# Two more quads with seven products in each ssm pass, left factors laid ready, and side transfers moved to ScalarE's and GpSimd's queues

## The chip, the core and the metric

The kernel runs on one core of a Trainium2 chip. A core has a matrix engine (TensorE, in profiles PE, its weight loads PEld), a vector engine (VectorE, DVE), a scalar engine (ScalarE, ACT), a general one (GpSimd, POOL) and a queue engine (SyncE, SP), which only issues transfers. Transfers (DMA) between device memory and on-chip memory can be issued from SP, ScalarE or GpSimd. Each engine takes its instructions in the order in which the compiler laid them, and waits where one needs another engine's or a transfer's result.

The metric is the device time of one execution in microseconds (us); lower is better.

## The reference

One layer of a hybrid block: 256 tokens, model width 2048, all in 32-bit floats. Cut to what matters here:

```python
hn = rms_norm(x, norm_w)
proj = hn @ w_in          # q k v z_a | z_s (4096) | xbc (6144) | dt (64) | g_a g_s
...                       # 16 heads of dilated attention -> o_a (256 x 2048)
xbc = silu(causal_depthwise_conv(xbc, conv_w, conv_b))
xs, bm, cm = split(xbc)   # xs: 64 heads of 64; bm, cm: 8 groups of 128
...                       # chunked scan over two chunks of 128 tokens -> y (256 x 4096)
y = rms_norm(y * silu(z_s), ssm_norm_w)
merged = sigmoid(g_a) * (o_a @ w_attn_branch) + sigmoid(g_s) * (y @ w_ssm_branch)
return rms_norm(x + merged @ w_out, final_norm_w)
```

The product `y @ w_ssm_branch` (256 x 4096 by 4096 x 2048) is what is meant by the ssm branch below.

## The kernel before, in words

All weights lie in device memory as one list of 481 *units* (`wall`), each 128 x 1024 floats, in the order of use (`weight_plan`). A unit is loaded by SP into a ring of five buffers (`w`), and then split into a high part `h` (ScalarE rounds it to the matrix engine's format, L276) and a low part `l` (VectorE subtracts, L277), four buffers each. A product of two split numbers takes three matmuls (high by high, high by low, low by high): a *triple*.

The stages in order: the first projections with the norm of x; then eight *groups* `g` of the ssm part. A group projects B and C (2 units each) and four pairs of xs and zs (2 units each), 20 units in all. Behind the projections run, with lags counted in *ticks* (one per projection of 2 units), the group's convolution, its `turn` (transposes of xs), four `decays` (each loads a broadcast of cumulated decays into the one buffer `acb` and fills a quarter of `gt`), and the `scan` (32 matmuls into `yp`, L820), after which `gather` puts the result into `yT`. Then come two passes of the ssm branch, two passes of v, the 16 attention heads (q, k, za), and two passes each for ga, attn and out.

A *pass* (`gemm_pair`) yields 1024 output columns. It walks over the inner dimension in *quads*: two blocks of 128 rows by two blocks of 512 columns, two weight units. The ssm passes have 16 quads, the others 8. A quad is done either plainly (24 matmuls of 128x512) or by Strassen's way with seven products (21 matmuls). `S_QUADS` names the latter. Such a quad needs
- sums and differences of the weights: T2 = B22 - (B12 - B11) and so on. Part of it (`wt`) can be made ahead: in `sum_jobs`, `get` loads a unit and a half unit of the quad, `add` makes two subtractions on VectorE (L252, L253), and `spill` stores the result to device memory (`presum`). The pass then loads `wt` (512 KB), `wa` (512 KB) and `wc` (256 KB). Otherwise the pass loads the second unit as `wb` and makes both differences itself (L549, L555). Quad 12 of both ssm passes is always done so (`IN_PLACE`).
- sums and differences of the left factor (`turn_x`): made ahead by `keep_left`, stored as `lefts`, and loaded again by `fetch_left` into an `sx` tile; or, for the quads of `Y_LATE`, made within the first ssm pass (`left_y`). Quads that both passes do with seven products store three of the four (`spare`).

For each seven quad ScalarE rounds four tiles (L543), and VectorE takes four differences of 1024 and one of 512 elements (L544, L557).

`behind_unit(n, f)` runs `f` right after unit n has been split. Before the change, each side transfer (a load of sums, of left factors, of constants) was tied to that place by a one-element copy on GpSimd (`gp.tensor_copy(dst[:, 0:1], behind)`, L247, L251, L432, L638, L903), which needs the unit's `h` and the free destination; SP (or ScalarE for the last loads of x and of the final weights) then issued the transfer. Stores by `spill` were SP's too. 18 differences fitted in the projections, at units 2, 9 and 16 of the groups 1 to 6 and made 3 units later: 13 for the ssm passes, 5 for v; four quads of the second v pass had none.

The compiler's scheduler lays the final order on each engine, by priorities and a timeline that it models; `high_priority(n)` puts an instruction n places ahead. `issue_after(ins)`, which the change uses, lets the instructions within follow `ins` on its engine, without a wait.

Of the kernel before, what the change touches and what calls it, by code (L numbers as in the profile page):

```python
# [15 lines left out]
P = 128  # L16
# [20 lines left out]
DT_LAG, CB_LAG, TURN_LAG, GT_LAG, Y_LAG, S_LAG, M_LAG = 2, 5, 3, 2, 11, 2, 2  # L37
# [3 lines left out]
V_ORDERS = {0: (0, 2, 4, 1, 3, 5, 6, 7), 2: (0, 2, 1, 4, 3, 5, 6, 7)}  # L41
# [6 lines left out]
    ("ssm", 0): (5, 7, 8, 10, 11, 12, 13), ("ssm", 2): (3, 5, 7, 8, 10, 11, 12, 13),  # L48
# [3 lines left out]
Y_ORDERS = {0: (0, 1, 2, 3, 5, 4, 7, 8, 6, 10, 11, 9, 12, 14, 13, 15), 2: (0, 3, 1, 5, 2, 7, 8, 4, 10, 11, 6, 12, 9, 13, 14, 15)}  # L52
Y_LATE = {12: 4, 13: 6}
# [9 lines left out]
SUM_UNITS = 2, 9, 16  # L63
# [133 lines left out]
def hybrid_block(ctx: ExitStack, tc: tile.TileContext, wall, xt, x, pk_d, cst_d, fw_d, out):  # L197
# [33 lines left out]

    def behind_unit(n, f):
        on_unit.setdefault(n, []).append(f)
# [4 lines left out]
    def spill(kept, key, name, src, shape):  # L238
        kept[key] = dram.tile([P, *shape], F32, name=name, tag=name)
        nc.sync.dma_start(kept[key], src)  # L240

    def sum_jobs(jobs, units, places):

        def get(tag, q, t, b11, behind):
# [5 lines left out]
        def add(tag, q, t, b11, res, behind):  # L250
            gp.tensor_copy(res[:, 0:1], behind)  # L251
            ve.tensor_tensor(res[:, :512], t[:, :512], b11, ALU.subtract)  # L252
            ve.tensor_tensor(res[:, 512:], t[:, 512:], res[:, :512], ALU.subtract)  # L253
            spill(presum, (tag, q), f"t_{tag[0]}{tag[1]}_{q}", res, [UNIT])

        for n, ((tag, q), u) in enumerate(zip(jobs, units)):
            t, b11, res = places[n % len(places)]
            behind_unit(u, lambda behind, a=(tag, q, t, b11): get(*a, behind))
            behind_unit(u + SUM_LAG, lambda behind, a=(tag, q, t, b11, res): add(*a, behind))
# [7 lines left out]
    def unit(n, shape):  # L267
# [6 lines left out]
        with tc.high_priority(L_AHEAD) if n >= KT // UB else nullcontext():  # L274
            for a, b in zip(cuts, cuts[1:]):
                ac.activation(h[:, a:b], w[:, a:b], AF.Copy)  # L276
                ve.tensor_tensor(l[:, a:b], w[:, a:b], h[:, a:b].bitcast(F32), ALU.subtract)  # L277
# [151 lines left out]
    def fetch_left(kept, pool, bufs, key, x, spare, u):  # L429
        def get(behind):  # L430
            sx = new_sx(pool, bufs, spare, f"{key[0]}{key[1]}")
            gp.tensor_copy(sx[:, 0, 0, 0:1], behind)  # L432
            nc.sync.dma_start(sx.bitcast(F32), lefts[key])
            kept[key[1]] = left_parts(sx, x, spare)
# [250 lines left out]
    with tc.tile_pool(name="ssm", bufs=2) as sp:  # L685
# [205 lines left out]
        for c in GS_BEFORE[0]:  # L891
# [3 lines left out]
        at = sums_at[:, 3]  # L895
# [3 lines left out]
            [(sums_at[:, 0], sums_at[:, 2, :512], sums_at[:, 1])],  # L899
        )  # L900

        def left_x(q, behind):
            gp.tensor_copy(at[:, 0:1], behind)  # L903
            keep_left(("x", q), two_kts(XT, q), 0, at)
# [4 lines left out]
        for g in range(GROUPS):  # L909
# [55 lines left out]
    xk = ctx.enter_context(tc.tile_pool(name="xk", bufs=1))  # L965
    sx_of_x = {}

    for n, q in enumerate(SX_X[:1]):
        fetch_left(sx_of_x, xk, 1, ("x", q), two_kts(XT, q), 0, plain_unit(("ssm", 2), 12, Y_ORDERS[2]))
# [7 lines left out]
    with tc.tile_pool(name="xp", bufs=1) as xp:  # L977
# [8 lines left out]
        for q in SX_Y:  # L986
            if q in Y_LATE:
                continue
            fetch_left(sxs, xp, sum(s == Y_SPARE[q] for s in Y_SPARE.values()), ("y", q), two_kts(yT, q), Y_SPARE[q], plain_unit(("ssm", 0), Y_ORDERS[0].index(q) - 3 if q in S_QUADS[("ssm", 0)] else 12, Y_ORDERS[0]))
# [24 lines left out]
    behind_unit(FIRST[("v", 2)] + 1, lambda behind: fetch(dc, cst_d[:, :768], behind))  # L1014
# [18 lines left out]
    with tc.tile_pool(name="att", bufs=2) as ap:  # L1033
# [33 lines left out]
        def mix(h, pT, za):  # L1067
# [10 lines left out]
            if h % 2 == 1 and q in ATT_QUADS:  # L1078
                keep_left(("o", q), two_kts(oaT, q), 0, mul.tile([P, UNIT], F32, name=f"sxt_o{q}", tag="ht", bufs=2))
# [3 lines left out]
            [  # L1083
                (th_a[:, i, :UNIT], th_a[:, 1, UNIT + 512 * i : UNIT + 512 * i + 512], th_a[:, 0, UNIT:])
                for i in range(2)
            ],
# [17 lines left out]
        for n, q in enumerate(ATT_QUADS):  # L1104
            fetch_left(
                sx_of_o, xl if n else xk, max(1, n and len(SX_X) - 1), ("o", q), two_kts(oaT, q), 0, FIRST[("ga", 2)] + O_BEHIND[n]
# [9 lines left out]
    with tc.tile_pool(name="fin", bufs=2) as fp:  # L1116
# [36 lines left out]
        for n in range(4):  # L1153
# [3 lines left out]
                lambda behind, i=i, cs=cs: fetch(fin[:, i, cs], x[i * P : (i + 1) * P, cs], behind, nc.scalar),  # L1157
# [3 lines left out]
        for n, (tag, u) in enumerate(FW_BEHIND):  # L1161
            cs = slice(n * UNIT, (n + 1) * UNIT)
            behind_unit(
                FIRST[tag] + u, lambda behind, cs=cs: fetch(fw[:, cs], fw_d[cs].partition_broadcast(P), behind, nc.scalar)
# [107 lines left out]
```

## Time and profile before

| What | us |
|---|---|
| Three runs | 1385.03, 1385.79, 1385.75 |
| Their median | 1385.75 |
| Profiled execution, from the first to the last instruction (span) | 1383.8 |
| Median above that span | 1.95 |
| Ssm passes, first matmul to the first of v | 583.6 to 748.5 |

The profile's page gives each engine's busy time, the span in 40 slices, the transfers by queue, the chain of work that ended last (followed back from the last instruction to what released each step), and the costliest groups of instructions. Other views of the same trace give the busy time in chosen stretches, instructions in order of time, and groups by line and shape. A matmul's record is longer (0.39 us) than the step from one to the next, because matmuls overlap; a busy TensorE can therefore still hide short waits, which show as a longer step. A few per cent of the matmul records may be missing.

### The profile page before, as it was taken

To read this page: it belongs to the slowest core of one execution; us is meant where nothing else is said; L and a number is where in the kernel's file an instruction comes from. 1 tells how busy PE (TensorE), PEld (TensorE's weight loads), DVE (VectorE), ACT (ScalarE), POOL (GpSimd) and SP (SyncE) were. 2 spreads that over 40 slices of the span, in tenths; PEclk is the share of its full clock that TensorE was granted. 3 is DMA by queue.
4 is the path that set the end of the run, shared out by engine and by line. 5 is a ranking of instruction groups with operands and counts; after the bars stand their busy time and mean duration, and the time that the engine had idled before them with its cause. 6 is when DMAs were issued, how large, how long until landed. Compare 5 with 4: busy or idle time off the path is not lost.

```text
span 1383.8 us, 20696 instructions
## 1 busy us (share of the span) xinstructions
PE 1373.6 (99%) x7266; PEld 1169.9 (85%) x7266; DVE 1169.5 (85%) x1753; ACT 835.5 (60%) x1306; POOL 142.0 (10%) x226
## 2 busy tenths in 40 slices
PE   9999999999999999999999999999999999999997
PEld 8888888888888888888888888888888888888886
DVE  7898999987799898789889897777877788888897
ACT  7656677675667675766565554544544556655564
POOL 2301111101011100010001001111111000000112
PEclk9999999999999999999999999999999999999999
DMA  9767988868787866668677668888888757865773
GB/s 347 231 187 225 313 254 291 279 224 287 245 266 240 294 212 208 188 224 280 230 259 267 222 209 278 275 275 273 299 288 301 241 161 264 294 222 180 243 273 122
DMA packets 105080, 345.00 MB, mean 249 GB/s; under 512 B 11728, under 2 KB 13712, under 8 KB 104976
## 3 DMA queue, kind: packets, MB, share of 16 engines
q1 hardware_dynamic: 103536, 339.62, 74.0%
q10 hardware_dynamic: 1440, 4.06, 0.8%
q8 instruction: 57, 0.93, 0.3%
q14 instruction: 47, 0.39, 0.1%
HBM read 314.87 MB, written 28.77 MB: 248 GB/s over the span
## 4 chain that ended last, share of the span: by engine, by line
PE 97%; DMA 1%; DVE 1%; ACT 1%; issue 0%; SPq 0%; POOL 0%; POOLq 0%; DVEq 0%; ACTq 0%
PE ps_zs L329 8%; PE ps_xs L329 8%; PE ps_zs L332 4%; PE ps_q L329 4%; PE ps_za L329 4%; PE ps_k L329 4%; PE ps_xs L332 4%; PE ps_ssm L476 3%; PE ps_ssm L477 3%; PE ps_ssm L478 3%; PE ps_q L332 2%; PE ps_k L332 2%; PE ps_za L332 2%; PE ps_gs L414 2%; PE ps_gs L412 2%; PE ps_gs L413 2%
## 5 line engine op out<-in xcount | busy, mean ns | idle before, releaser
L276 ACT ACTIVATE h<-w 128x1024 fp32r<-128x1024 f32 (+1 forms) x398 | 413.9, 1047 | 318.0 <-issue 78.8
L277 DVE TENSOR_TENSOR l<-w,h 128x1024 fp32r<-128x1024 f32 (+1 forms) x398 | 479.4, 1211 | 124.2 <-ACT h L276 121.8
L329 PE MATMUL ps_zs<-XT,h 128*128 128x512 f32 x496 | 176.3, 397 | 0.0
L329 PE MATMUL ps_xs<-XT,h 128*128 128x512 f32 x496 | 175.9, 396 | 0.0
L332 PE MATMUL ps_zs<-XT,l 128*128 128x256 f32 x496 | 139.9, 282 | 0.0
L332 PE MATMUL ps_xs<-XT,l 128*128 128x256 f32 x496 | 139.8, 282 | 0.0
L329 PEld LDWEIGHTS ps_xs<-XT,h 128*128 128x128 f32 x496 | 93.3, 188 | 21.7
L329 PEld LDWEIGHTS ps_zs<-XT,h 128*128 128x128 f32 x496 | 93.4, 188 | 21.2
L332 PEld LDWEIGHTS ps_zs<-XT,l 128*128 128x128 f32 x496 | 93.7, 189 | 1.5 <-issue 0.7
L332 PEld LDWEIGHTS ps_xs<-XT,l 128*128 128x128 f32 x496 | 93.7, 189 | 0.4
L329 PE MATMUL ps_q<-XT,h 128*128 128x512 f32 x256 | 92.5, 405 | 0.2 <-ACT h L276 0.2
L329 PE MATMUL ps_k<-XT,h 128*128 128x512 f32 x256 | 89.9, 395 | 0.0
L329 PE MATMUL ps_za<-XT,h 128*128 128x512 f32 x256 | 89.7, 394 | 0.0
L543 ACT ACTIVATE ha<-wa 128x1024 fp32r<-128x1024 f32 x43 | 45.4, 1055 | 46.4 <-DMA wa<-in_wall 10.9
L332 PE MATMUL ps_q<-XT,l 128*128 128x256 f32 x256 | 71.2, 278 | 0.0
L332 PE MATMUL ps_k<-XT,l 128*128 128x256 f32 x256 | 71.1, 278 | 0.0
L332 PE MATMUL ps_za<-XT,l 128*128 128x256 f32 x256 | 71.1, 278 | 0.0
L544 DVE TENSOR_TENSOR la<-wa,ha 128x1024 fp32r<-128x1024 f32 x43 | 52.5, 1220 | 11.9 <-ACT ha L543 11.8
L782 ACT ACTIVATE gt<-acb,acT 128x128 f32<-128x128 f32 x128 | 44.2, 391 | 23.7 <-DMA acb<-acum_d 21.9
L329 PEld LDWEIGHTS ps_q<-XT,h 128*128 128x128 f32 x256 | 48.2, 188 | 11.5 <-ACT h L276 0.6
L329 PEld LDWEIGHTS ps_za<-XT,h 128*128 128x128 f32 x256 | 48.1, 188 | 11.3
L329 PEld LDWEIGHTS ps_k<-XT,h 128*128 128x128 f32 x256 | 48.1, 188 | 11.2
(688 smaller groups left out, 3325.1 us busy)
## 6 DMA issues: line engine op xcount, KB each, us to landing
w<-in_wall SPq DMA_DIRECT2D x394, 512.0 KB, 4.7
wa<-in_wall SPq DMA_DIRECT2D x43, 512.0 KB, 4.9
th_a<-in_wall SPq DMA_DIRECT2D x19, 512.0 KB, 5.6
sums_at<-in_wall SPq DMA_DIRECT2D x18, 512.0 KB, 4.7
acb<-acum_d SPq DMA_DIRECT2D x32, 256.0 KB, 4.0
t_ssm<-sums_at SPq DMA_DIRECT2D x13, 512.0 KB, 4.1
wt<-t_ssm SPq DMA_DIRECT2D x13, 512.0 KB, 5.4
th_a<-in_wall SPq DMA_DIRECT2D x19, 256.0 KB, 6.0
```

The lines of the kernel that those rows point to most:

```text
L276: ac.activation(h[:, a:b], w[:, a:b], AF.Copy)
L277: ve.tensor_tensor(l[:, a:b], w[:, a:b], h[:, a:b].bitcast(F32), ALU.subtract)
L329: pe.matmul(acc, h[:, kk, :], m, start=(kt == 0), stop=False)
L332: pe.matmul(acc[:, S:], l[:, kk, :], m[:, :S], start=False, stop=(kt == KT - 1))
L412: pe.matmul(accs[i], xh, h[:, kk], start=(kt == 0), stop=False)
L413: pe.matmul(accs[i], xh, l[:, kk], start=False, stop=False)
L476: pe.matmul(acc, xh, h, start=start, stop=False)
L477: pe.matmul(acc, xh, l, start=False, stop=False)
L478: pe.matmul(acc, xl, h, start=False, stop=stop)
L543: ac.activation(h, src, AF.Copy)
L544: ve.tensor_tensor(l, src, h.bitcast(F32), ALU.subtract)
L782: ac.activation(g4[:, n, b], acb[:, j, b // 2 * P : b // 2 * P + P], AF.Relu, scale=-1.0, bias=sc[:, h : h + 1],)
```

## The change

- The ssm passes do 9 (first) and 10 (second) of their 16 quads with seven products, where they did 7 and 8: quads 6 and 9 are added to both. The orders of the quads are new, also that of the first v pass.
- `sum_jobs` has five places a group instead of three, so all 26 differences of ssm and v are made in the projections. The result is made in the tile into which the unit was loaded (no third tile), and there are two such places.
- Loads of sums, of left factors and of constants are issued by ScalarE (`side`), behind the unit's `h`, and the subtractions follow the unit's `l` on VectorE; the one-element copies on GpSimd go. Stores by `spill` are issued by GpSimd.
- All four left factors of x are fetched at the beginning of the v passes (one had been fetched in the second ssm pass, into a pool of its own).
- The decays of a group come 2, 4, 6 and 9 ticks behind its last xs projection instead of 2, 3, 4 and 9; those of the last group start with the projection before. The last scan comes 4 ticks after the last xs projection (11 before), the one before it 7.

```diff
-DT_LAG, CB_LAG, TURN_LAG, GT_LAG, Y_LAG, S_LAG, M_LAG = 2, 5, 3, 2, 11, 2, 2
+DT_LAG, CB_LAG, TURN_LAG, Y_LAG, S_LAG, M_LAG = 2, 5, 3, 11, 2, 2
+GT_LAGS, END_LAGS, END_LAG = (2, 4, 6, 9), (2, 3, 4, 5), (7, 4)
-V_ORDERS = {0: (0, 2, 4, 1, 3, 5, 6, 7), 2: (0, 2, 1, 4, 3, 5, 6, 7)}
+V_ORDERS = {0: (0, 1, 2, 4, 3, 5, 6, 7), 2: (0, 2, 1, 4, 3, 5, 6, 7)}
-    ("ssm", 0): (5, 7, 8, 10, 11, 12, 13), ("ssm", 2): (3, 5, 7, 8, 10, 11, 12, 13),
+    ("ssm", 0): (5, 6, 7, 8, 9, 10, 11, 12, 13), ("ssm", 2): (3, 5, 6, 7, 8, 9, 10, 11, 12, 13),
-Y_ORDERS = {0: (0, 1, 2, 3, 5, 4, 7, 8, 6, 10, 11, 9, 12, 14, 13, 15), 2: (0, 3, 1, 5, 2, 7, 8, 4, 10, 11, 6, 12, 9, 13, 14, 15)}
-Y_LATE = {12: 4, 13: 6}
+Y_ORDERS = {0: (0, 1, 2, 5, 6, 3, 7, 8, 4, 9, 10, 14, 11, 12, 13, 15), 2: (0, 1, 3, 5, 2, 6, 7, 4, 8, 9, 14, 10, 11, 12, 13, 15)}
+Y_LATE = {12: 3, 13: 4}
-SUM_UNITS = 2, 9, 16
+SUM_UNITS = 1, 5, 9, 13, 17
...
+    def side(dst, src, queue=nc.scalar):
+        with tc.issue_after(here["high"]):
+            queue.dma_start(dst, src)
...
     def spill(kept, key, name, src, shape):
         kept[key] = dram.tile([P, *shape], F32, name=name, tag=name)
-        nc.sync.dma_start(kept[key], src)
+        gp.dma_start(kept[key], src)
...
-            for dst, src in ((t, wall[n + 1]), (b11, wall[n, :, :512])):
-                gp.tensor_copy(dst[:, 0:1], behind)
-                nc.sync.dma_start(dst, src)
+            side(t, wall[n + 1])
+            side(b11, wall[n, :, :512])
...
-            gp.tensor_copy(res[:, 0:1], behind)
-            ve.tensor_tensor(res[:, :512], t[:, :512], b11, ALU.subtract)
-            ve.tensor_tensor(res[:, 512:], t[:, 512:], res[:, :512], ALU.subtract)
-            spill(presum, (tag, q), f"t_{tag[0]}{tag[1]}_{q}", res, [UNIT])
+            with tc.issue_after(here["low"]):
+                ve.tensor_tensor(t[:, :512], t[:, :512], b11, ALU.subtract)
+                ve.tensor_tensor(t[:, 512:], t[:, 512:], t[:, :512], ALU.subtract)
+            spill(presum, (tag, q), f"t_{tag[0]}{tag[1]}_{q}", t, [UNIT])
...
-            [(sums_at[:, 0], sums_at[:, 2, :512], sums_at[:, 1])],
+            [(sums_at[:, n], sums_at[:, 3, n * 512 : n * 512 + 512]) for n in range(2)],
...
+                if t == 4 * GROUPS - 2:
+                    for k in range(4):
+                        after(1 + k, lambda a=(g, k, cb, state): decays(*a))
...
-                    y_lag = Y_LAG + gate
-                    for k in range(4):
-                        after(GT_LAG + k if k < 3 else y_lag - 2, lambda a=(g, k, cb, state): decays(*a))
+                    y_lag = ((Y_LAG,) * (GROUPS - 2) + END_LAG)[g] + gate
+                    for k, lag in enumerate(END_LAGS if g == GROUPS - 2 else GT_LAGS):
+                        if g < GROUPS - 1:
+                            after(lag + gate // 2, lambda a=(g, k, cb, state): decays(*a))
...
-            fetch_left(sx_of_x, vx, len(SX_V), ("x", q), two_kts(XT, q), 0, FIRST[("v", 0)])
-        for n, q in enumerate(SX_X[1:]):
-            fetch_left(sx_of_x, xl, len(SX_X) - 1, ("x", q), two_kts(XT, q), 0, FIRST[("v", 0)] + 1 + n)
+            fetch_left(sx_of_x, vx, len(SX_V), ("x", q), two_kts(XT, q), 0, FIRST[("v", 0)] + 3)
+        for n, q in enumerate(SX_X):
+            fetch_left(sx_of_x, xl, len(SX_X), ("x", q), two_kts(XT, q), 0, FIRST[("v", 0)] + n)
...
-                lambda behind, i=i, cs=cs: fetch(fin[:, i, cs], x[i * P : (i + 1) * P, cs], behind, nc.scalar),
+                lambda behind, i=i, cs=cs: side(fin[:, i, cs], x[i * P : (i + 1) * P, cs]),
```

More of the change, by code (lines that the diff above doesn't have):

```diff
@@ L431, in get @@
             sx = new_sx(pool, bufs, spare, f"{key[0]}{key[1]}")
-            gp.tensor_copy(sx[:, 0, 0, 0:1], behind)
-            nc.sync.dma_start(sx.bitcast(F32), lefts[key])
+            side(sx.bitcast(F32), lefts[key])
             kept[key[1]] = left_parts(sx, x, spare)
@@ L988, in hybrid_block @@
                 continue
-            fetch_left(sxs, xp, sum(s == Y_SPARE[q] for s in Y_SPARE.values()), ("y", q), two_kts(yT, q), Y_SPARE[q], plain_unit(("ssm", 0), Y_ORDERS[0].index(q) - 3 if q in S_QUADS[("ssm", 0)] else 12, Y_ORDERS[0]))
+            fetch_left(sxs, xp, sum(s == Y_SPARE[q] for s in Y_SPARE.values()), ("y", q), two_kts(yT, q), Y_SPARE[q], plain_unit(("ssm", 0), max(Y_ORDERS[0].index(q) - 3, 0) if q in S_QUADS[("ssm", 0)] else 12, Y_ORDERS[0]))
         for c in (0, 2):
@@ L1078, in mix @@
             if h % 2 == 1 and q in ATT_QUADS:
-                keep_left(("o", q), two_kts(oaT, q), 0, mul.tile([P, UNIT], F32, name=f"sxt_o{q}", tag="ht", bufs=2))
+                last = q == ATT_QUADS[-1]
+                place = ring(f"sxt_o{q}") if last else mul.tile([P, UNIT], F32, name=f"sxt_o{q}", tag="ht", bufs=2)
+                keep_left(("o", q), two_kts(oaT, q), 0, place)
         sum_jobs(
             SUMS_ATT, range(FIRST[("q", 0)] + 7, N_UNITS, ATT_EVERY),
[L1083 to L1086, printed above, removed]
+            [(th_a[:, i, :UNIT], th_a[:, i, UNIT : UNIT + 512]) for i in range(2)],
         )
@@ L1163, in hybrid_block @@
             behind_unit(
-                FIRST[tag] + u, lambda behind, cs=cs: fetch(fw[:, cs], fw_d[cs].partition_broadcast(P), behind, nc.scalar)
+                FIRST[tag] + u, lambda behind, cs=cs: side(fw[:, cs], fw_d[cs].partition_broadcast(P))
             )
```

28 lines of the change are left out of this document (13 added, 15 removed).

## The prediction, made before the changed kernel had run

> **What bounds the kernel now.** I read the page's engine shares first, then the chain that ended last, then the busy time by stretches, then the two places where TensorE and VectorE meet. The page says that one engine is busy throughout, and its chain says that this engine is the path:
>
> ```profile
> span 1383.8 us, 20696 instructions
> PE 1373.6 (99%) x7266; PEld 1169.9 (85%) x7266; DVE 1169.5 (85%) x1753; ACT 835.5 (60%) x1306; POOL 142.0 (10%) x226
> ...
> PE 97%; DMA 1%; DVE 1%; ACT 1%; issue 0%; SPq 0%; POOL 0%; POOLq 0%; DVEq 0%; ACTq 0%
> ```
>
> So a matmul less is time less, as long as nothing new makes TensorE wait; and no other engine's saving counts by itself. The stretches show how much room the others have. Columns: the stretch, its length, then busy time and instruction count of PE, PEld, DVE, ACT, POOL, then the granted clock, the DMA share and GB/s.
>
> ```profile
> 0.00:30.00 30.00, 28.26 (x140) 24.14 (x141) 21.66 (x36) 22.94 (x40) 6.93 (x15) 1.00 0.93 337
> ...
> 110.00:564.00 454.00, 454.00 (x2687) 391.82 (x2686) 400.04 (x650) 311.17 (x590) 48.72 (x99) 1.00 0.78 255
> 600.00:740.00 140.00, 140.00 (x620) 115.97 (x619) 121.06 (x127) 85.18 (x93) 2.28 (x4) 1.00 0.77 259
> 583.00:660.00 77.00, 77.00 (x350) 63.71 (x346) 65.53 (x81) 48.52 (x56) 4.79 (x7) 1.00 0.74 248
> 660.00:742.00 82.00, 82.00 (x364) 67.93 (x363) 72.21 (x76) 47.73 (x54) 0.29 (x1) 1.00 0.76 253
> 742.00:824.00 82.00, 82.00 (x363) 67.81 (x362) 74.83 (x81) 44.00 (x51) 5.27 (x5) 1.00 0.64 220
> 180.00:240.00 60.00, 60.00 (x368) 52.22 (x367) 57.18 (x95) 43.20 (x84) 8.56 (x17) 1.00 0.85 278
> 380.00:440.00 60.00, 60.00 (x362) 51.77 (x361) 54.25 (x91) 40.89 (x80) 7.96 (x15) 1.00 0.79 261
> ```
>
> 110 to 564 are the projections (groups 1 to 7), 583 to 742 the two passes of the ssm branch, 742 to 824 most of the two v passes. TensorE has no gap in any of them, at full clock. VectorE is next: 88% in the projections, but 95% in group 2 (180 to 240) and 88% in the second ssm pass. One place shows TensorE really waiting, at the end of the v passes:
>
> ```profile
> 824.03 0.67 PE L476 MATMUL pp_v<-tl_v,sx_x 128*128 128x512 f32 x2
> 824.90 0.50 PE L329 MATMUL ps_q<-XT,h 128*128 128x512 f32 x1 [0.20 <-ACT h L276]
> ...
> 813.42 0.69 DVE L549 TENSOR_TENSOR wb<-wb,wa 128x512 f32<-128x512 f32 x1 [1.94 <-DMA wb<-in_wall]
> ```
>
> **The change, part by part.**
>
> *Matmuls.* A plain quad is two units of 2 x 2 triples, 24 matmuls; a quad with seven products has 7 triples, 21. The first ssm pass gets quads 6 and 9, the second 6 and 9: 4 quads x 3 = 12 matmuls of 128x512 go. In 600 to 740 TensorE does nothing else: 620 instructions touch the stretch; matmuls of 0.39 us overlap, so some 1.7 of them count for the edge, and 140.00 / 618.3 = 0.2264 us each. 12 x 0.2264 = **-2.72 us**, all on the path.
>
> *The wait at 824.* Two matmuls start from 824.03, so the second at about 824.26 to 824.30, and the next starts at 824.90: 0.6 us for a step of 0.23, so 0.38 lost. VectorE was late there because the four quads of the second v pass had no difference laid ready: it subtracts twice more per quad, and one load into the ring came late (the 1.94 above). After the change all 26 differences of ssm and v are made in the projections (6 groups x 5 places; 18 were made there before). These rows price VectorE's work (columns: line, engine, operation, shapes, count | busy us, mean ns | idle before):
>
> ```profile
> L277 DVE TENSOR_TENSOR l<-w,h 128x1024 fp32r<-128x1024 f32 x390 | 474.1, 1221 | 122.6 <-ACT h L276 120.1
> L544 DVE TENSOR_TENSOR la<-wa,ha 128x1024 fp32r<-128x1024 f32 x43 | 52.5, 1220 | 11.9 <-ACT ha L543 11.8
> L252 DVE TENSOR_TENSOR sums_at<-sums_at 128x512 f32<-128x512 f32 x18 | 12.4, 690 | 1.0 <-DMA sums_at<-in_wall 0.2
> L549 DVE TENSOR_TENSOR wb<-wb,wa 128x512 f32<-128x512 f32 x6 | 4.1, 688 | 3.2 <-DMA wb<-in_wall 3.2
> L450 DVE TENSOR_TENSOR sums_at<-sums_at 128x128 f32<-128x128 f32 x11 | 3.1, 285 | 0.0
> ...
> 724.51 2.36 DVE L277 TENSOR_TENSOR l<-w,h 128x1024 fp32r<-128x1024 f32 x2
> ```
>
> Two 1024-wide ones in a row take 2.36, so the second starts 1.14 after the first; the same 0.08 off leaves 0.61 for 512 and 0.21 for 128. The second v pass is freed of 4 x 2 x 0.61 = 4.9 us: 742 to 824 falls from 74.83 to 69.9 of 82 (85%). I take the wait as gone: **-0.38 us**; bounds 0 (it moves) and -0.5 (with the slow step after it).
>
> *VectorE in the ssm passes.* A seven quad costs it 4 x 1.14 + 0.61 = 5.17, a plain one 2 x 1.14 = 2.28. Two more per pass: +5.8. First pass (583 to 660): 71.3 of 75.6, 94%. Second: 72.21 + 5.8 = 78.0 of 80.6, 97%; its order now has four seven quads in a row (10, 11, 12, 13), each of 5.17 against 21 x 0.2264 = 4.75 of TensorE, so it falls behind by 1.7 over the four, and by 1.2 more for quad 12, whose differences are still made on the spot. h and l have 4 buffers each, so VectorE may be several units ahead beforehand. I cost this at nothing; cover is that lead; without it, 2.9 us.
>
> *VectorE in the projections.* 8 more differences x 2 x 0.61 = 9.8, left factors of quads 6 and 9 at 0.61 + 4 x 0.21 and two low parts, at most 0.61 + 0.21, = 2.3 each: 400.04 + 14.4 = 414 of 454, 91%. By group it is narrower: 57.18 + 2.4 = 59.6 of 60 in 180 to 240, and 54.25 + 2.4 + 2.3 = 59.0 of 60 in 380 to 440. Against it stands that part of the present lag comes from queues that the change relieves. In 380 to 440 ScalarE stands 2.56 for a broadcast of decays, and SP holds weight loads behind it and behind stores that wait for VectorE:
>
> ```profile
> 392.11 0.70 ACT L782 ACTIVATE gt<-acb,acT 128x128 f32<-128x128 f32 x2 [2.56 <-DMA acb<-acum_d]
> ...
> L240 SPq EVENT_SEMAPHORE  x47: 17/17/1898, 121.6 to 1130.2; - x47
> L240 SPq DMA_DIRECT2D t_ssm<-sums_at x13: 326/327/945, 123.3 to 394.4; - x13
> L639 ACTq DMA_DIRECT2D fin<-in_x x4: 335/352/353, 1287.1 to 1335.4; - x4
> ```
>
> The four decays of a group were issued 2, 3, 4 and 9 ticks behind it, now 2, 4, 6 and 9, so the one buffer acb is refilled with a tick between. I take 0 for the projections, between 0 (TensorE has no gap there to win) and +7.1 (all the added work of both tight groups, 2.4 + 4.7).
>
> *Queues.* Off SP: 74 loads of sums_at and th_a, 15 of left factors, dc, 37 + 15 stores, at 0.33 each some 47 us of issue, and their waits (the longest 1.9). On ScalarE: 2 x 45 sum loads, 17 left factors, dc = 108 at 0.35 = 38 us over the kernel, 52 x 0.35 = 18 in the projections: 311.17 to 329 of 454, 73%. ScalarE is not late there, so 0; cover is its lead over VectorE. On POOL: 62 stores, and the tiny copies that tied each load to a unit go. No row shows a transfer issued by POOL. The nearest: a POOL copy, and a store that SP issues.
>
> ```profile
> L251 POOL COPY th_a<-h 128x1 f32<-128x1 f32 x19 | 23.6, 1241 | 157.8 <-ACT h L276 157.8
> ...
> t_ssm<-sums_at SPq DMA_DIRECT2D x13, 512.0 KB, 4.1
> sums_at<-in_wall SPq DMA_DIRECT2D x18, 512.0 KB, 4.7
> ...
> 489.23 2.75 PE yp L820 x32
> 549.85 2.75 PE yp L820 x32
> 580.90 2.75 PE yp L820 x32
> ```
>
> For the price of a store, from 1.24 for the issue and 4.1 to land, I take 5.3 us; for the path, bounds 0 (POOL's 142 us of work are hidden now) and the second rival below. A group is 549.85 - 489.23 = 60.6 us for 20 units, 3.03 a unit. A place for sums is used every 8 units, 24.2 us; the subtraction comes 3 units after the load, so a store may land 15.1 us after it before a load waits. 5.3 is far below: I take 0.
>
> The load has a new way to hurt: it waits on ScalarE's own queue for its place, and every h behind it waits too, then l, then TensorE. Before, POOL took that wait.
>
> *Traffic.* 8 x 1.3 MB sums, 4 quads with a 256 KB piece more in ssm and four in v, two left factors: +14 MB on 345, mostly from 110 to 564: 255 to about 282 GB/s, 337 being moved in the first 30 us. 0.
>
> The Trainium skill (DMA: Bandwidth & Descriptors, "Issuing engines are not separate DMA queues") says that transfers of all issuing engines run on the same 16 DMA engines, so that another issuer saves sequencer time only. By that rule the moves are worth what SP's issue and waits are worth, which on this path is 0 too, and the added traffic is not hidden by a second queue.
>
> *The last scan.* The last scan (at 580.90, the last thing before the ssm pass) comes 4 ticks after the last projection, and its decays earlier still. TensorE does the same 2.75 us sooner. Cover: VectorE's gaps in the last gates. 0; if its inputs are late, up to 2.75.
>
> **Sum.** -2.72 - 0.38 = -3.10 against the profiled execution: span 1383.8 to 1380.7. The median of the three runs is 1385.75, 1.95 above that span; 1385.75 - 3.10 = **1382.65**, so 1382.6. This is 0.22%; below 0.2% (2.77 us) a measurement of this kernel can hardly tell a change from none, so the forecast lies just beyond that line.
>
> **Rivals.**
>
> *VectorE gives part of it back (within 0.2%).* For: 97% in the second ssm pass, 98 and 99% in two groups. In 660 to 742 it idled 82 - 72.21 = 9.8 us; only 2.6 would be left. If half of the old idle time is waiting for h that can't be squeezed, 4.9 - 2.6 = 2.3 us of stall: 1385.0. If only the row of four seven quads pays, 2.9 less 2 of lead (an estimate: under one unit, 12 x 0.2264 = 2.7), 1383.5. Against: TensorE did not wait once in 180 to 240 at 95%, and VectorE's idle time is mostly waiting for h, whose buffers TensorE frees.
>
> *ScalarE is held by a side load (slower).* Place: the sum loads of the projections, each waiting for POOL's store out of the same place. It decides once a store lands later than 15.1 us after its subtraction. At 15.6 every round of a place grows by 0.5; 26 sums on two places are 13 rounds, 6.5 us: 1382.6 + 6.5 = 1389.1. Against: it takes about three times the 5.3 above.
>
> The Trainium skill (SBUF — State Buffer, "SBUF: two separate sides", the box on VectorE blocking DMA) says that a transfer issued from GpSimd has its descriptors written by GpSimd, which is locked out while VectorE runs copies in a two-port mode; it advises the ScalarE or SP queue instead. By that rule this rival would come true if VectorE's work were such copies. The rows above agree with it only in that VectorE is busy; they are all TENSOR_TENSOR, which the same page says has no such mode.
>
> *The wait at 824 only moves* (seven quads in a row in the first v pass now): -2.72 alone, 1383.0, counted with the first rival.
>
> **How the numbers follow.** Forecast 0.53, VectorE giving back 0.29, held ScalarE or a like stall over 6 us 0.18. So faster 0.53, same 0.29, slower 0.18. The forecast's own range is 1381.9 (the wait, the slow step and smaller stalls all gone, -3.9) to 1383.0. The range reaches up through the first rival to 1388.0 and leaves out the slower case: 1381.9 to 1388.0.
>
> **What would show it.** Right: 12 matmuls fewer in the ssm passes, 600 to 740 still at 0.226 a matmul, no TensorE gap at the end of v, no wb in v, VectorE at 95 to 98% in the second ssm pass. Wrong: idle time of PE before ps_ssm or ps_xs released by l, lc or ltu (first rival), or ScalarE's h released by the landing of a POOL store (second). The forecast fails if either exceeds 0.3 us in sum, or if POOL's transfers lengthen the end.

## The result: slower by 1.1%, and the profile after

The changed kernel takes 1401.45 us (median of four runs, 1397.66 to 1402.4) against 1385.48 for the kernel before beside it: a ratio of 1.0108, interval 1.0095 to 1.0122. 1382.6 was forecast, in a range of 1381.9 to 1388.0. The profiled execution has a span of 1399.0 us, 15.2 more than before. Its page, with the engines' busy time, and the shares of the chain that ended last by engine and (in part) by line:

```profile
span 1399.0 us, 20543 instructions
PE 1376.1 (98%) x7254; PEld 1167.5 (83%) x7254; DVE 1183.1 (85%) x1787; ACT 845.4 (60%) x1318; POOL 76.8 (5%) x150
...
PE 83%; DMA 5%; DVE 5%; ACT 3%; issue 2%; SPq 0%; POOL 0%; ACTq 0%; POOLq 0%; DVEq 0%
```

The 12 matmuls are gone (7266 to 7254), but TensorE's part of the chain fell from 97% to 83%: it now waits for transfers, VectorE and ScalarE. The stretches show that it has gaps where it had none:

```profile
110.00:564.00 454.00, 448.80 (x2664) 387.06 (x2663) 407.65 (x676) 315.22 (x602) 26.31 (x79) 1.00 0.81 278
180.00:240.00 60.00, 57.27 (x344) 48.95 (x343) 54.15 (x90) 40.73 (x79) 4.24 (x12) 1.00 0.87 307
380.00:440.00 60.00, 60.00 (x364) 52.02 (x363) 54.97 (x93) 42.13 (x81) 4.60 (x12) 1.00 0.89 318
590.00:665.00 75.00, 73.18 (x320) 60.17 (x319) 62.61 (x74) 45.53 (x53) 1.63 (x1) 0.98 0.74 248
665.00:755.00 90.00, 87.40 (x376) 69.35 (x375) 78.90 (x81) 53.46 (x59) 0.00 (x0) 1.00 0.72 242
```

TensorE's waits in the projections are three; they sum to the 5.2 us that are missing from its 454 (who waited for what: us, times, longest):

```profile
PE ps_xs L335 <- ACT h L282: 2.5, 1, 2.5
PE ps_xs L338 <- DVE l L283: 1.5, 1, 1.5
PE ps_zs L335 <- ACT h L282: 1.2, 1, 1.2
```

The granted clock is 1.00 in the projections, so it is not the clock there. Later, apart from the last microseconds of either kernel, it fell twice, each time about the end of a long wait of TensorE (1.82 us until 633.8, 2.98 until 1136.5; columns as in the stretches above):

```profile
634.50:637.90 3.40, 3.40 (x10) 2.62 (x9) 3.38 (x4) 0.72 (x1) 0.00 (x0) 0.51 0.62 227
1136.20:1139.60 3.40, 3.08 (x9) 2.52 (x10) 3.40 (x6) 2.74 (x5) 0.53 (x1) 0.50 0.20 40
```

A matmul then takes a step of 0.43 us and not 0.23, which adds some 1.5 us to each of these waits. Not every long wait brings it (the 2.47 until 458 does not); why, the runs do not show.

In 180 to 240 VectorE is *less* busy than before (54.15 against 57.18) while TensorE waits: something holds both.

A table of the stages, from the starts of their first matmuls in the profiled executions (one a kernel), is the measure for all that follows. "Projections" reach from the first matmul of B1 to the first of the ssm passes, "passes" from there to the first of v, "v and attention" on to the first of ga, and "ga" to the first of attn.

| Kernel (profiled execution) | span | projections | passes | v and attention | ga |
|---|---|---|---|---|---|
| before | 1383.8 | 472.9 | 165.0 | 372.8 | 83.6 |
| changed | 1399.0 | 478.0 | 171.0 | 373.4 | 87.4 |
| old quads | 1395.0 | 478.7 | 164.8 | 373.3 | 87.7 |
| 18 differences | 1395.7 | 472.3 | 165.9 | 379.9 | 87.5 |
| old decays | 1396.4 | 478.7 | 168.9 | 373.3 | 86.1 |
| last scratch in ht | 1393.1 | 477.8 | 167.7 | 372.2 | 85.6 |
| no subtractions | 1392.7 | 473.6 | 168.3 | 373.4 | 87.5 |
| subtractions only | 1389.2 | 472.0 | 167.8 | 373.3 | 86.1 |
| scratch as second buffer | 1408.8 | 484.3 | 171.8 | 373.3 | 88.7 |
| all side transfers on SP | 1403.3 | 484.4 | 166.9 | 374.6 | 87.3 |
| differences by POOL in the passes | 1419.3 | 472.6 | 196.6 | 372.2 | 87.8 |
| wt, wc loaded by POOL | 1400.5 | 477.6 | 168.6 | 375.6 | 87.7 |
| no lu | 1395.8 | 480.4 | 165.0 | 373.4 | 86.1 |
| quads alone, on before | 1400.8 | 472.6 | 173.9 | 380.5 | 83.6 |
| three parts undone | 1386.1 | 472.5 | 164.8 | 372.8 | 85.6 |
| and store by SP | 1384.4 | 472.5 | 164.8 | 372.9 | 83.6 |
| one quad a pass | 1386.8 | 473.4 | 165.3 | 374.6 | 83.6 |
| old quads, 4 a group | 1387.1 | 476.2 | 164.8 | 372.2 | 83.6 |

The loss thus has three places: projections +5.2, passes +6.0 (8.7 above the forecast), ga +3.8. Where a stage's code is the same, the changed kernels scatter: 477.6 to 480.4 in the projections, 165.9 to 171.8 in the passes. Smaller differences there say nothing. Part of the scatter is the clock: it fell to 0.5 in the passes of the two kernels with 171.0 and 171.8, and not in those with 165.9 to 168.9. In ga, with the same wait of 2.97 to 2.99 us, it fell in the seven kernels with 87.3 to 88.7 and not in the three with 86.1. Without a waiting TensorE the stages agree to 0.2 us (164.8 four times).

*The projections.* The chain of work around the first stall (start, duration, what):

```profile
169.00 7.84 DMA acb<-acum_d
...
178.76 5.85 DMA acb<-acum_d
...
186.50 0.95 ACT h L282
187.50 0.50 PE ps_zs L335
```

The broadcast of the decays lands 7.84 and 5.85 us after its start. ScalarE, which takes its instructions in order, waits for it with the next unit's h queued behind, and TensorE waits for that h. All of ScalarE's waits for it in 110 to 584, in the kernel before and in the changed one (us, times, longest):

```profile
ACT gt L782 <- DMA acb<-acum_d: 21.9, 18, 2.6
ACT gt L787 <- DMA acb<-acum_d: 28.9, 18, 3.1
```

The kernel before thus waited three quarters as long and lost nothing. In the changed one two of TensorE's waits (1.2 at 187, 2.5 at 458) end a chain from the broadcast, and the third (1.5 at 202) ends with VectorE's l. The landings, the first row from the page of the kernel before (transfer, count, KB, median us):

```profile
acb<-acum_d SPq DMA_DIRECT2D x32, 256.0 KB, 4.0
...
w<-in_wall SPq DMA_DIRECT2D x386, 512.0 KB, 4.8
...
t_ssm<-sums_at POOLq DMA_DIRECT2D x17, 512.0 KB, 6.6
...
acb<-acum_d SPq DMA_DIRECT2D x32, 256.0 KB, 4.9
```

ScalarE also stood for POOL's stores out of the place that a side load wanted, in the same stretch:

```profile
ACT lo_x L389 <- DMA t_ssm<-sums_at: 2.5, 2, 1.4
ACT h L282 <- DMA t_ssm<-sums_at: 2.4, 1, 2.4
```

Of the 24 rounds in which a place was used again, 11 loads were issued 0.02 to 0.03 us after the store before them had landed; in the kernel before none was, nor in any kernel with three or four differences a group.

*The passes.* The chain at the stalls near 631 and 746:

```profile
625.01 7.58 DMA wa<-in_wall
...
632.70 1.06 ACT ha L548
...
633.80 0.50 PE pp_ssm L481
...
741.58 1.23 DVE ltu L549
...
742.83 4.35 DMA w<-in_wall
...
747.21 1.06 ACT h L282
...
748.31 0.73 PE ps_ssm L481 x2
```

VectorE's last operation (at 746 the subtraction ltu, at 631 one for a left factor, sx_y) frees a place, the load into it starts 0.02 us later, and after the load and ScalarE's rounding TensorE goes on: a loop around five places with no slack left in it at these two points.

*The start of ga.* TensorE, in order of time (start, duration, what, idle before and releaser):

```profile
1133.14 0.40 PE L483 MATMUL pp_ga<-htt,sx_x 128*128 128x512 f32 x1
1136.52 0.45 PE L1070 MATMUL ptp<-cst,p 128*128 128x128 f32 x1 [2.98 <-DVE p L1065]
```

The transpose of the last head's softmax stands ahead of nearly all of ga: 7 matmuls of ga come before the last of its transposes, against 36 in the kernel before, whose time hid the softmax.

### The profile page after: what moved, and what is told of

It reads as the page before. It is cut to its first block, busy times and chain, and to the rows that moved or that the text cites. A ratio compares the mean times of both kernels' runs of the same rounds, so it can differ in the third digit from the quotient of the medians.

```text
span 1399.0 us, 20543 instructions
## 1 busy us (share of the span) xinstructions
PE 1376.1 (98%) x7254; PEld 1167.5 (83%) x7254; DVE 1183.1 (85%) x1787; ACT 845.4 (60%) x1318; POOL 76.8 (5%) x150
## 4 chain that ended last, share of the span: by engine, by line
PE 83%; DMA 5%; DVE 5%; ACT 3%; issue 2%; SPq 0%; POOL 0%; ACTq 0%; POOLq 0%; DVEq 0%
PE ps_zs L335 7%; PE ps_xs L335 7%; PE ps_za L335 4%; PE ps_k L335 4%; PE ps_q L335 4%; PE ps_zs L338 4%; PE ps_xs L338 3%; DMA acb<-acum_d 3%; PE ps_q L338 2%; PE ps_za L338 2%; PE ps_k L338 2%; PE ps_gs L418 2%; PE ps_gs L420 2%; PE ps_gs L419 2%; PE ps_out L481 2%
## 5 line engine op out<-in xcount | busy, mean ns | idle before, releaser
L282 ACT ACTIVATE h<-w 128x1024 fp32r<-128x1024 f32 (+1 forms) x390 | 405.8, 1047 | 295.0 <-issue 63.1
L283 DVE TENSOR_TENSOR l<-w,h 128x1024 fp32r<-128x1024 f32 (+1 forms) x390 | 469.5, 1209 | 119.1 <-ACT h L282 117.8
L548 ACT ACTIVATE ha<-wa 128x1024 fp32r<-128x1024 f32 x47 | 49.6, 1056 | 36.9 <-DMA wa<-in_wall 12.9
L549 DVE TENSOR_TENSOR la<-wa,ha 128x1024 fp32r<-128x1024 f32 x47 | 57.3, 1220 | 13.4 <-ACT ha L548 13.2
L787 ACT ACTIVATE gt<-acb,acT 128x128 f32<-128x128 f32 x128 | 44.2, 391 | 33.2 <-DMA acb<-acum_d 28.9
L548 ACT ACTIVATE htu<-wa 128x1024 fp32r<-128x1024 f32 x42 | 44.3, 1054 | 22.6 <-DVE wa L562 9.8
```

Of the source, the lines that this page charges most:

```text
L282: here["high"] = ac.activation(h[:, a:b], w[:, a:b], AF.Copy).ins
L283: here["low"] = ve.tensor_tensor(l[:, a:b], w[:, a:b], h[:, a:b].bitcast(F32), ALU.subtract).ins
L548: ac.activation(h, src, AF.Copy)
L549: ve.tensor_tensor(l, src, h.bitcast(F32), ALU.subtract)
L787: ac.activation(g4[:, n, b], acb[:, j, b // 2 * P : b // 2 * P + P], AF.Relu, scale=-1.0, bias=sc[:, h : h + 1],)
```

## The experiments

The changed kernel is the base unless another is named.

**Each part undone.** First the quads:

```diff
-("ssm", 0): (5, 6, 7, 8, 9, 10, 11, 12, 13), ("ssm", 2): (3, 5, 6, 7, 8, 9, 10, 11, 12, 13)
+("ssm", 0): (5, 7, 8, 10, 11, 12, 13), ("ssm", 2): (3, 5, 7, 8, 10, 11, 12, 13)
 ... and Y_ORDERS, Y_LATE as before
```

> The changed kernel with the ssm passes' old quads (7 and 8 with seven products), old orders and old late left factors; queues, decays, last scan and the rest as changed. Theory 1 (work: seven-product quads ask more of VectorE than TensorE's time for them, and a late VectorE frees the ring's places late): the two ssm passes go from 170.8 us back to the 164.7 of before, the projections gain 1 to 2 us from four differences fewer; 1393 to 1395 in all. Theory 2 (queues: the moved side transfers make the ring's loads late): the passes stay at 168 us or more and the total at 1397 or more.

1396.92 us, ratio to before 1.0077 (1.0062 to 1.0092), above the 1393 to 1395 of theory 1. The passes are back at 164.8 without a stall, so their loss is the quads' and not the queues'. The projections did not gain: 22 differences at five a group cost as much as 26.

```diff
-SUM_UNITS = 1, 5, 9, 13, 17
+SUM_UNITS = 2, 9, 16
```

> The changed kernel with 18 differences made in the projections (3 places in a group, as before) instead of 26; eight of the v passes' quads then make theirs on the spot. Theory 1 (work): the projections give back at least 3 of their 5.2 us of loss; the v passes pay 1 to 4 us for 8 x 2 differences of 0.61 us there; 1397 to 1400. Theory 2 (the decays' new spacing and their one broadcast buffer cause the loss): the projections stay within 1 us of the changed kernel's, and the total is 1401 to 1405.

1398.07 us, 1.0101 (1.0076 to 1.0125). The projections' loss is gone in full (472.3), and v pays 6.5 us for its eight quads, more than I expected. That fits theory 1, but this kernel has fewer transfers too, so it does not tell VectorE's work from them.

```diff
-for k, lag in enumerate(END_LAGS if g == GROUPS - 2 else GT_LAGS):
+for k, lag in enumerate((2, 3, 4, y_lag - 2)):
     if g < GROUPS - 1:
-        after(lag + gate // 2, ...)
+        after(lag, ...)
```

> The changed kernel with the decays' old spacing for groups 0 to 6 (2, 3, 4 and 9 ticks behind the group); the last group as changed. Theory 2 (decays): the projections give back 4 us or more, 1396 to 1397.5. Theory 1 (work): less than 1 us, 1400.5 to 1402.

1402.34 us, 1.0115 (1.0096 to 1.0134): projections 478.7 (in its fastest run, 1398.17, which was the profiled one). The decays' spacing is not it; stalls of the same kind stand at the same places (187, 202, 457).

```diff
-place = ring(f"sxt_o{q}") if last else mul.tile(...)
+place = mul.tile(...)
```

> The changed kernel with the scratch of the last attention left factor (quad 6) in the buffer ht as before, not in a place of the weight ring. If the place held in the ring keeps the weight loads of the gate projection ga back: the 4.4 us of stalls at 1131 to 1139 go, nothing else moves, 1397.0 to 1397.5. If the stall is the order that was fixed at build time for other reasons (queues, left factors kept elsewhere): it stays, 1401 to 1402.

1396.83 us, 1.0084 (1.0065 to 1.0102). With the scratch out of the weight ring 36 matmuls of ga stand before that transpose again, and the 3 us at 1133 go; but ga still has 85.6 against 83.6, with a new stall:

```profile
1138.21 6.36 DMA sxd_o<-sxt_o
...
1144.65 1.07 ACT htu L548
...
1145.74 1.24 DVE ltu L549
...
1147.02 0.50 PE pp_ga L482
```

POOL's store out of the buffer ht holds ScalarE, which wants that buffer.

**VectorE's work or the transfers?** Two kernels that take one and leave the other.

```diff
-with tc.issue_after(here["low"]):
-    (the two subtractions of add)
+if tag[0] not in ("ssm", "v"):
+    with tc.issue_after(here["low"]): (the two subtractions)
```

> The changed kernel with the 26 x 2 subtractions in the projections left out (so the quads with seven products get a wrong difference); the loads and stores around them stay. Time from the first matmul of B1 to the first of the ssm passes is 472.9 us before, 478.0 changed. Theory V (VectorE's added work): it falls to 474 or less, 1396.5 to 1398. Theory D (the added transfers delay the broadcast of the decays, for which ScalarE waits in order): it stays at 476 or more, 1399.5 or more.

1394.15 us, 1.006 (1.0045 to 1.0075): projections 473.6.

```diff
 n = FIRST[tag] + 2 * q
+if tag[0] in ("ssm", "v") and len(got) > 1:
+    return
+got.append(n)
 ... and add stores only the first result
```

> The opposite: the 26 x 2 subtractions in the projections stay, but only the first two differences are loaded and the first stored, the others left out (all quads read that one, a wrong difference): 25 stores of 512 KB and 24 loads of 768 KB fewer. Theory D (transfers): from B1 to the ssm passes falls from 478.0 to 474 us or less, 1396 to 1398. Theory V (VectorE): stays at 476 or more, 1399.5 or more.

1392.42 us, 1.0047 (1.0032 to 1.0062): projections 472.0. Taking away either load brings back nearly the whole, so both theories met their sign. The stretch of this kernel, its waits for the broadcast, and the broadcast's landing on its page:

```profile
110.00:564.00 454.00, 454.00 (x2690) 392.31 (x2690) 414.34 (x686) 317.95 (x608) 12.80 (x54) 1.00 0.69 211
```

```profile
ACT gt L795 <- DMA acb<-acum_d: 13.4, 13, 3.1
```

```profile
acb<-acum_d SPq DMA_DIRECT2D x32, 256.0 KB, 4.0
```

VectorE does 414.34 us of 454, the whole added work, and TensorE has no gap; with the transfers at 211 GB/s instead of 278 the waits for the broadcast fall from 28.9 to 13.4. Without the subtractions (the kernel ahead of it) they hardly fall, and yet little is lost; its stretch and its waits:

```profile
110.00:564.00 454.00, 453.18 (x2683) 391.21 (x2683) 384.86 (x631) 317.46 (x607) 26.35 (x79) 1.00 0.83 281
```

```profile
ACT gt L788 <- DMA acb<-acum_d: 25.5, 19, 2.6
```

Either load alone is covered, or nearly; both together are not. My reading is that late transfers make the waits and that VectorE, with 91% of its time taken, has too little lead to cover them; through which steps the two act together is not shown. Both kernels also take away ScalarE's waits for POOL's stores (none is left in either), and the second also 48 issues of ScalarE, so they do not part these from the two theories. The waits for stores are not needed for the first two stalls: in the kernel with the old decays ScalarE first idles for one at 210 us, after the stalls at 187 and 202. What they add is open.

```diff
-acb = sp.tile([P, 2, S], F32, name=f"acb{t}", tag="acb", bufs=1)
+acb = sums_at[:, 2, 512:] (as 2 x S) if i % 2 else sp.tile(...)
```

> The changed kernel with a second buffer for the broadcast of the decays (the odd ones go to the upper half of the scratch for left factors). If the one buffer, refilled 5 to 8 us before ScalarE may go on, is where either load reaches TensorE: B1 to the ssm passes falls from 478.0 to 474 us or less, the stalls near 186, 200 and 455 go, 1396.5 to 1398. If the lead is lost elsewhere and the broadcast is only the last in the row: 476 or more.

1409.56 us, 1.0171 (1.0148 to 1.0194), projections 484.3: a miss. The scratch is not free often enough; SP now waits for stores out of it, with weight loads behind (`SPq L785 <- DMA sxd_y<-sums_at: 21.1, 7, 4.6`). It tells nothing of a second buffer with room of its own, which no run tried.

```diff
-def side(dst, src, queue=nc.scalar):
+def side(dst, src, queue=nc.sync):
-gp.dma_start(kept[key], src)
+nc.sync.dma_start(kept[key], src)
```

> The changed kernel with the side loads and the stores issued by SP, as before, the rest as changed. Theory Q (the moves to ScalarE's queue and to POOL cost the time): B1 to the ssm passes falls from 478.0 to 475 us or less and the passes from 170.8 to 168 or less, 1394 to 1397. Theories V and D: no gain, since the same work and the same bytes remain, 1400 to 1406 with SP fuller than in the changed kernel.

1406.27 us, 1.0143 (1.0123 to 1.0163), projections 484.4. The projections speak against theory Q: with the side transfers back on SP they take 6.4 us more (some 2.5 of it from a granted clock of 0.5 over the 5.1 us behind a wait of 3.9). The 166.9 of the passes, below its 168, lies within their scatter. But the wait for a free place has only moved with the loads: SP, with weight loads behind it, stands 90.7 us for the stores in 110 to 584, of which for those of the ssm passes (us, times, longest):

```profile
SPq L237 <- DMA t_ssm<-sums_at: 63.3, 16, 6.1
```

So this kernel does not show that such waits are free on ScalarE. SP's stores land no sooner than POOL's did (page):

```profile
t_ssm<-sums_at SPq DMA_DIRECT2D x17, 512.0 KB, 7.1
```

**The passes.**

```diff
-IN_PLACE = {"ssm": [(0, 12), (2, 12)]}
+IN_PLACE = {"ssm": (all seven quads of both passes)}
-    ve.tensor_tensor(wt[...], ..., ALU.subtract)   # both differences
+    gp.tensor_tensor(wt[...], ..., ALU.subtract)
 ... SUM_UNITS = 5, 13; last scratch in ht
```

> The changed kernel with the differences of all 19 seven-product quads of the ssm passes made there by POOL (two subtractions of 128x512 a quad, from a second raw load into the ring), so that only the 9 of v are made in the projections; and the scratch of the last attention left factor in ht. In the projections 17 differences and their 17 x 1.25 MB go. Theory D and V alike: B1 to the ssm passes falls from 478.0 to 473 us or less. In the passes 19 loads of 256 KB go, VectorE's work stays, and each quad waits for POOL once more: if the passes lose time because the ring's loads come late, they fall below 169 us; if a POOL subtraction of this size takes over 2 us, they rise above 175. Total 1388 to 1394 if POOL is quick, over 1398 if not.

1420.26 us, 1.0254 (1.0239 to 1.027): projections 472.6 as expected, passes 196.6. POOL's price for a difference (count | busy, mean ns | idle before):

```profile
L561 POOL TENSOR_TENSOR wb<-wb 128x512 f32<-128x512 f32 x19 | 33.3, 1752 | 38.9 <-DVE lc L549 37.3 <-DMA wb<-in_wall 1.7
L555 POOL TENSOR_TENSOR wb<-wb,wa 128x512 f32<-128x512 f32 x19 | 32.4, 1703 | 135.9 <-DMA wb<-in_wall 109.9 <-DVE la L549 14.8 <-DVE l L283 5.8
```

1.70 to 1.75 us is below the 2 us that I had set as the limit, yet the passes rose by 25.6: as I read it, two such steps in a row lengthen the ring's loop, which had no slack (POOL itself mostly waits, 109.9 us for the load of wb).

```diff
-nc.sync.dma_start(wt, presum[tag, q])
-nc.sync.dma_start(wc, wall[n + 1, :, 512:])
+gp.dma_start(wt, ...)   # in the ssm passes
+gp.dma_start(wc, ...)
```

> The changed kernel with the ssm passes' loads of the ready differences (wt) and of the quarter wc issued by POOL and not by SP, where they wait for their places ahead of the ring's other loads (33 us at wc alone). Theory S (SP stands behind those waits, so the loads of wa and w start late): the passes fall from 171.0 to 166 us or less, 1395 to 1397. Theory L (VectorE frees the places late, whoever issues): they stay at 168 or more, 1399 to 1402.

1401.94 us, 1.0129 (1.0106 to 1.0153): passes 168.6, within the scatter of passes left alone. SP's order is not shown to matter.

```diff
-part(wa, hu, lu)
+ac.activation(hu, wa, AF.Copy); lu = lt   # in the ssm passes
```

> The changed kernel with one of VectorE's 128x1024 operations left out in each seven-product quad of the ssm passes (the low part of the last factor, for which the one before is used: a wrong value): 19 x 1.14 us of VectorE's work. Theory L (VectorE's 5.17 us a quad against 4.75 of TensorE): the stalls of the passes go and they take 162.5 to 164 us, 1391 to 1394. Theory S (SP's order of loads): they stay at 167 or more.

1397.38 us, 1.0104 (1.0071 to 1.0136). Passes 165.0, lower than any with these quads and full work (165.9 to 173.9); steps over 0.15 us too long sum to 1.8 us against 3.0 to 8.9. VectorE's load over the passes, in two halves:

```profile
592.40:675.00 82.60, 82.60 (x369) 68.16 (x368) 63.25 (x75) 54.51 (x63) 1.63 (x1) 1.00 0.78 265
675.00:757.30 82.30, 81.11 (x353) 65.64 (x352) 64.18 (x67) 49.71 (x57) 0.00 (x0) 1.00 0.69 242
```

The first pass has no gap any more at 77% VectorE. This points to theory L, but from one profile, 0.9 below the lowest of the others: 162.5 to 164 was expected, and the end of the second pass still waits. What the last 2.7 us above the prediction's 162.3 are is open.

> The kernel before with the seven-product quads, the orders and the late left factors of the changed kernel, and what they need of room (the left factors of x fetched by v, with v's new first order); queues, 18 differences in the projections, decays and last scan as before. If the loss in the passes belongs to the quads: passes 166 to 171 us against 165.0, projections as before (472.9), eight quads of v make their differences on the spot and pay 4 to 6 us; 1390 to 1397. If it belongs to the moved queues: passes 162 to 163, and 1387 to 1390.

(The kernel before with the quads, orders and late left factors above, and all left factors of x in one pool.) 1401.69 us, 1.0117 (1.0102 to 1.0133): projections 472.6, ga 83.6, passes 173.9, v 7.7 more than before: above the expected 1390 to 1397. The quads alone lose in the passes, more than among the changed queues; ga's loss is not theirs.

**Do the parts add up?** Old quads, 18 differences and the scratch in ht at once:

> The changed kernel with three parts undone: the ssm passes' old quads and orders, 18 differences in the projections, the last attention scratch in ht. Queues, decays' spacing and last scan stay changed. If the three losses add up and the rest costs nothing: B1 to the ssm passes 472.3 to 473.0 us, passes 164.9, ga 85.6, in all 1386 to 1388. If something else of the change costs too: over 1389.

1388.41 us, 1.0019 (1.001 to 1.0028), 0.4 above the expected range. The profiled span is 1386.1: three undone parts take away 12.9 us. The last 2 us of ga then, with the same order on the engines, and the chain of this kernel:

```profile
1130.90 6.30 DMA sxd_o<-sxt_o
...
1137.29 1.06 ACT htu L548
```

```diff
-gp.dma_start(kept[key], src)
+(nc.sync if key[0] == "o" else gp).dma_start(kept[key], src)
```

> The same, and the four stores of the attention left factors are issued by SP again and not by POOL. If the 2 us that remain in ga are ScalarE's wait for POOL's store out of the buffer ht (landing 6.4 us after 1138.2): ga falls from 85.6 to 83.6 us and the total to 1384.5 to 1386, the same as before. If the store only comes late because its data do: ga stays at 85 or more.

1385.74 us, 1.0001 (0.9992 to 1.001): ga 83.6, and the kernel is where the one before was. The same store, alone in a window from 1130.5 to 1132:

```profile
sxd_o<-sxt_o SPq DMA_DIRECT2D x1, 512.0 KB, 4.3
```

Issued by POOL it took 6.3 us, and ga those 2.0 us more. What is left of the change (queues, decays, last scan) is worth nothing that can be measured, with three differences a group.

> The kernel of the store by SP with one seven-product quad a pass more than before (6; 9 stays plain), the changed orders, and 24 differences in the projections at 4 a group. Two quads, 6 matmuls less: 1.4 us. If four such quads in a row (10 to 13 with 9 ahead) are what VectorE cannot follow: passes 163 to 164 us. If each seven-product quad beyond the old ones costs: 165.5 to 168. In the projections as in the next kernel.

(S_QUADS without quad 9; SUM_UNITS 2, 7, 12, 17.) 1388.8 us, 1.0021 (1.0013 to 1.003): passes 165.3, with 3.3 us of long steps; 163 to 164 was expected if only the row of quads from 9 on were at fault, 165.5 to 168 if each quad costs. One more quad a pass already loses what it saves; v and attention, at 374.6, lose another 1.8 that no run explains.

> The kernel of the store by SP with all 22 differences of the old quads made in the projections, at 4 a group (3 lose nothing, 5 lose 5 to 6 us). If the loss grows with the transfers' rate from the first one on: B1 to the ssm passes 474.5 to 476 us, 1386 to 1388.5. If there is slack that only 5 a group exceeds: 472.3 to 473.5, and with no difference left to make in the v passes 1384 to 1385.5.

(Old quads; SUM_UNITS 2, 7, 12, 17.) 1387.94 us, 1.0016 (1.0007 to 1.0024): projections 476.2, 0.2 above the first range, with one stall of 2.6 at 461; the kernel ahead, with the same four a group, has 473.4. Against 472.5, three differences a group cost nothing, four 0.9 and 3.7 us, five 5.1 to 7.9 (the six kernels with all their work). The loss begins between three and four. At four it is not the broadcast that decides, but one late weight load behind VectorE, the loop of the ssm passes (its chain):

```profile
453.47 1.01 DVE l L283
454.49 7.90 DMA w<-in_wall
...
463.58 0.50 PE ps_zs L335
```

The v passes without differences to make save 0.6 (372.2 against 372.8), far less.

No version beat the kernel before.

## Why the prediction was wrong, step by step

- *Matmuls, -2.72.* Right in the count; the saving drowned in the waits.
- *Wait at 824, -0.38.* Right: from the first matmul of v to the last q projection the changed kernel is 0.6 faster, and the wait came back wherever v had four differences to make (0.38 and 0.40 in the two kernels with three parts undone).
- *Traffic, 0.* This step failed for the projections. I held a mean (282 GB/s forecast, 278 measured) against the 337 of the first 30 us. But what counts is the landing time of single transfers for which an engine waits in order: two of the three stalls (3.7 of the 5.2 us) end with the broadcast of the decays, whose landing rose from a median of 4.0 to 4.9 us, up to 7.84. The prediction had the row of that wait (2.56 at 392) and did not price it. The Trainium skill (DMA: Bandwidth & Descriptors, "Issuing engines are not separate DMA queues"), cited there, says that transfers of all issuers interleave on the same engines; the runs fit that (cutting the transfers and leaving the subtractions took the broadcast from 4.9 to 4.0 us), and I had drawn the wrong conclusion from it.
- *VectorE in the projections, 0 between 0 and +7.1.* The work was sized right (414 of 454: 414.34 where only it was added) and hidden when alone. Taken together with the transfers it was not: +5.2. I priced the two apart, and each fitted.
- *VectorE in the ssm passes, 0 with 2.9 uncovered.* This failed most: 8.7 above the forecast (some 1.5 of it the clock behind the stall at 631), 0.9 to 6.8 above before in the kernels with these passes among the changed queues. I took as the price the work by which VectorE exceeds TensorE. But a late VectorE frees a ring place late, and the load into it (4.4 to 7.6 us in the chain) comes on top of its lag. The first rival named the place, with 2.3 us.
- *Last attention scratch in the ring, not costed at all.* It held weight loads of ga back and changed the order at build time: some 3 us (the scratch in ht brought 1.2 in v and attention and 1.8 in ga, some 1.5 of these the clock behind the 2.98).
- *Queues, 0; POOL's store 5.3 us.* It landed after 6.6 (median), but the 15.1 allowed for it was not there. That figure put the subtraction 3 units, 9 us, behind the issue of its load; it ended 9 to 24 us behind it (9 to 18 in the kernel before, whose places came round later). So 11 of 24 loads stood for the store, and the second rival (ScalarE held by POOL's store) did come true in the projections: ScalarE idled 4.9 us for stores of the ssm passes' differences. The rival gave this 6.5 us; none of the three stalls is released by it, and what it adds to them is open. Its mechanism showed alone at the start of ga, where the next use of the buffer followed at once: 2.0 us. The same lag is hidden or fatal by who comes next.
- *Last scan, 0.* Right: the two kernels with 18 differences and old quads have 472.5 against 472.9.

## What to carry to other kernels

When an edit adds work and transfers that each fit under the same lead, price them together: look for the transfer that an in-order engine waits for, and ask how late it lands under the new load, not whether the mean rate stays under a peak. Take the time of a round through a buffer (load, work, store) from the trace and not from the planned order. Where buffers go round in a ring, an engine that falls behind pays the load's latency on top of its lag, so "97% busy, covered by the lead" can be a loss and not a tie. A buffer borrowed from a ring and a store moved to another issuer must be checked at the one place where their next user comes at once.

## What the runs showed of the hardware

The same 512 KB store landed 6.3 us after its issue by POOL and 4.3 after one by SP, at the same place in the same order. The Trainium skill (DMA: Bandwidth & Descriptors, "Specifications") gives a first-byte latency of about 1 us for the GpSimd path and 0.6 for SP's and ScalarE's: the sign agrees, the 2.0 measured here is five times the 0.4 by that page, but it is a landing and not a first byte, and one pair of stores (the medians of the four in each kernel are 5.5 and 4.1). The Trainium skill (SBUF — State Buffer, "SBUF: two separate sides") warns that VectorE in a two-port mode locks GpSimd out of writing descriptors. Nothing like it could be seen beside this kernel's subtractions: with VectorE at 90% POOL's stores of differences landed in 6.6 us, and SP's, in the kernel with all side transfers on SP, in 7.1. A subtraction of 128x512 took 1.70 to 1.75 us on POOL, beside VectorE's own work, against 0.69 on VectorE. The granted clock read 0.5 for 3.4 us about the end of waits of TensorE of 1.82 and 2.98 us in the changed kernel, and a matmul then took a step of 0.43 us and not 0.23.
